# A new order for the start stage of a two-layer diffusion trunk: the first modulation group computed in halves

## The chip, the cores and the metric

The kernel runs on one core of one Trainium2 chip. The metric is the time of one execution in microseconds (us), measured on the device. TensorE multiplies matrices (PE; its weight loads are shown apart as PEld), VectorE (DVE), ScalarE (ACT) and GpSimd (POOL) compute, SyncE (SP) issues most transfers.

## The reference, cut to what matters

Two request groups (128 prompt tokens, 256 latent tokens) pass through two layers of width 1024, each a SwiGLU block, a token mixer and a second SwiGLU block. Before each block the tokens are normalised and modulated; `shift` and `scale` come from the conditioning vector by one large linear map:

```python
def modulate_norm(x, g, shift, scale):
    return rms_norm(x, g) * (1.0 + scale[:, None, :]) + shift[:, None, :]

m = (jax.nn.silu(cond) @ mod_w[l] + mod_b[l]).reshape(cond.shape[0], N_MOD, D_MODEL)
hf = modulate_norm(x, g[0], m[:, 0], m[:, 1])
x = x + FFN_RES * m[:, 2, None] * rms_norm(swiglu(hf, ffn_w1[l, 0], ffn_w2[l, 0]), g[1])
```

Only the very first use of this, up to the first three column units of the first `h @ w1`, lies in the code that is changed.

## The kernel before, in words

The 384 tokens are three tiles of 128 (tile 0 prompt, tiles 1 and 2 latent). All large products are fp32 in three passes: an operand is split into a high part (an ACT copy to fp32r, "hi", line 152 or 154 for weights, 431 for activations) and the rest (a DVE subtraction, "lo", lines 155 and 432). `mm3` (445 to 447) issues hi x hi, hi x lo of the activations, and lo of the weights x hi, so its third pass needs the weights' lo part.

Weights stream through four raw buffers of 1 MB; a unit is cast in two halves into three hi/lo buffers (`prep`). `release` gives a buffer back, `half` (`weights` in the start stage) casts the next one. With `"all"`, `prep` hands back four steps instead of doing them: hi and lo of the first 512 columns (`parts[u][0]`, `[1]`) and of the second 512 (`[2]`, `[3]`).

`start` (from line 721) handles what comes before the pipeline is full. It lies in a region of manual order (`order_begin`), in which every engine takes its instructions in the order of the program text. The code of `__init__` lies outside it. The stage consists of:

- statistics of each token tile: two ACT squares with a sum (331), then on DVE and ACT the reciprocal root (`rstd_of`, 310 to 322; the square root is ACT line 309), then the scaled tile `xn` (384 on DVE, 385 on ACT);
- `transposed(t)`: eight PE transposes (391) into two banks, copied out (765) by DVE and ACT;
- four modulation groups `g` of 256 columns each for shift and scale: `mods` (788, PE), `rows` (796, a DVE copy), `vectors` (801, PE, with the DVE steps 809 and 811 that make the vectors), `evac` (840 on DVE and 842 on ACT, then the split 431 and 432). Group `g` gives the row blocks k = 2g and 2g + 1 of the activations;
- `products(g, u)`: twelve matmuls of unit u for these two blocks, both halves (gate, up) of the unit. Groups 0 and 1 use the unit's first weight half (group 0 its first 512 columns, group 1 its second), groups 2 and 3 the second weight half;
- `keep_warm` (771): products of the identity with itself whose result nobody reads.

The order written out by hand after the transposes is, in short: `vectors(0)`, `evac(0)`, the casts of all three units, `products(0, 0)`, `products(0, 1)`, the second part casts, `mods(1)`, half of `products(0, 2)`, `vectors(1)`, `evac(1)`, the other half, `mods(2)`, `products(1, 0)`, `vectors(2)`, `evac(2)`, `next_weights(0)`, `products(1, 1)`, `next_weights(1)`, `products(1, 2)`, `mods(3)`, `next_weights(2)`, `products(2, 0)`, `vectors(3)`, `evac(3)`, `products(2, 1)`, `products(2, 2)`, and `products(3, u)`.

Of the kernel before, what the change touches and what calls it, by code (L numbers as in the profile page):

```python
# [19 lines left out]
P = 128  # L20
D = 1024
# [8 lines left out]

RAW_BUFS = 4
HALF_BUFS = 3
WARM, WARM2 = 10, 10
TAIL = 5


class Trunk:
    def __init__(self, ctx, tc, io):
        self.ctx, self.tc, self.nc, self.io = ctx, tc, tc.nc, io
        nc = self.nc  # L40
        pool = lambda name, bufs=1, **kw: ctx.enter_context(tc.tile_pool(name=name, bufs=bufs, **kw))
        self.cp = pool("const")
        self.sp = pool("small", 2)
        self.wp = pool("weights")
        self.pp = pool("psum", 1, space=bass.MemoryType.PSUM)
        self.dp = pool("scratch", 1, space=bass.MemoryType.DRAM)
        self.uid = 0

        const = lambda name, shape: self.cp.tile(shape, F32, tag=name, name=name)
        cc = const("cc", [P, KC, 2])  # L50
        nc.sync.dma_start(cc, io["cond"])
        self.x = const("x", [P, NT, D])
        for t in range(NT):
            src = io["x_prompt"] if t == 0 else io["x_sample"][(t - 1) * P : t * P]
            nc.sync.dma_start(self.x[:, t, :], src)
        self.nwT = const("nwT", [P, 6, KC])
        nc.gpsimd.dma_start(self.nwT, io["norm_pre"])
        self.mbT = const("mbT", [P, 6, 3, KC])
        nc.gpsimd.dma_start(self.mbT, io["mod_bT"])
        self.npT = const("npT", [P, 6, KC])  # L60
        nc.gpsimd.dma_start(self.npT, io["norm_post"])
        self.sel = const("sel", [P, 2])
        nc.gpsimd.dma_start(self.sel, io["sel"])
        self.csT = const("csT", [P, KC, 32])
        nc.vector.memset(self.csT, 0.0)
        self.cc = cc
        self.ident = const("ident", [P, P])
        make_identity(nc, self.ident)
        self.one = const("one", [P, 1])
        nc.vector.memset(self.one, 1.0)  # L70
        self.xh = self.cp.tile([P, KC, TOK], F32R, tag="xh", name="xh")
        self.xl = self.cp.tile([P, KC, TOK], F32R, tag="xl", name="xl")
        self.gates, self.shift, self.scale = {}, {}, {}
        self.gate_rows = {}
        self.cond_rows = None
# [295 lines left out]
    def stat_steps(self, t):  # L371

        nc = self.nc
        st = {}

        square, eps, sums = self.square_steps([self.x[:, t, 0:512], self.x[:, t, 512:1024]])

        def rstd():
            eps()
            st["z"] = self.rstd_of(**sums)  # L380

        def scale(tag="xn"):
            xn = self.cp.tile([P, D], F32, tag=tag, name=self.name("xn"))
            nc.vector.tensor_scalar(xn[:, 0:512], self.x[:, t, 0:512], st["z"], None, op0=ALU.mult)
            nc.scalar.activation(xn[:, 512:], self.x[:, t, 512:], AF.Copy, scale=st["z"])
            return xn

        return square, rstd, scale, eps
# [336 lines left out]
    def start(self, units):  # L725
# [3 lines left out]
        with self.tc.tile_pool(name="start", bufs=1, reuse_waits="tile") as tp:  # L729
            raw0 = {}  # L730

            def load(g):
                for v in range(2):
                    raw0[g, v] = tp.tile([P, KC, 256], F32, tag=f"m0_{g}_{v}", name=f"m0_{g}_{v}")
                    nc.sync.dma_start(raw0[g, v], io["mod_first"][g, v])
# [5 lines left out]
                    self.loaded += 1  # L741
                nc.sync.dma_start(self.raw[u][0][:, c0:c1], self.unit_src(units[u])[0][:, c0:c1])

            load(0)
            for g in range(2):
                for u in range(3):
                    load_part(u, 512 * g, 512 * (g + 1))
                load(g + 1)
            load_part(0, D, 2 * D)
            load(3)  # L750
            load_part(1, D, 2 * D)
# [22 lines left out]
            def squares(t):  # L774
                for h in (1, 0):
                    stats[t][0](h)

            vec = [self.mod_vec(v) for v in range(2)]
            self.shift[0], self.scale[0] = vec
            ws, sums, rowsof = {}, {}, {}  # L780
# [17 lines left out]
            def vectors(g, *vs):  # L798
                po = self.psum(1)
                for i in range(2 * vs[0], 2 * vs[-1] + 2):  # L800
                    nc.tensor.matmul(po[:, 2 * i : 2 * i + 2], rowsof[g][:, i * P : (i + 1) * P], self.sel,  # L801
                                     start=True, stop=True)
                for v in vs:
                    for j in range(2):
                        k = 2 * g + j
                        src = po[:, 4 * v + 2 * j : 4 * v + 2 * j + 2]
                        b = self.mbT[:, 0, v, k : k + 1]
                        if v == 0:
                            nc.vector.tensor_scalar(vec[0][:, :, k], src, b, None, op0=ALU.add)
                        else:  # L810
                            nc.vector.tensor_scalar(vec[1][:, :, k], src, b, self.nwT[:, 0, k : k + 1],
                                                    op0=ALU.add, op1=ALU.mult)

            squares(0), stats[0][1]()
            squares(1)
            xn0 = stats[0][2]()
            stats[1][1]()
            squares(2)
            xn1 = stats[1][2]("ptmp")
            nc.vector.tensor_scalar(self.nwT, self.nwT, RS, None, op0=ALU.mult)  # L820
            for j in range(6):
                nc.vector.tensor_scalar(self.mbT[:, j, 1, :], self.mbT[:, j, 1, :], 1.0, None, op0=ALU.add)
            stats[2][1]()
            transposed(0, xn0)
            xn2 = stats[2][2]()
            transposed(1, xn1)
            mods(0, 0)
            rows(0, 0)
            transposed(2, xn2)
            mods(0, 1)  # L830
            parts = {0: self.prep(1, "all")}
            parts[0][0]()
            rows(0, 1)
            banks = [self.psum(b) for b in (6, 7, 4, 5, 2, 3)]

            def evac(g, between=None):
                for j in range(2):
                    k = 2 * g + j
                    tmp = self.cp.tile([P, D], F32, tag=("xn", "ptmp")[j], name=self.name("xtmp"))[:, :TOK]
                    nc.vector.tensor_scalar(tmp[:, 0:P], xnT[:, k, 0:P], vec[1][:, 0, k : k + 1],  # L840
                                            vec[0][:, 0, k : k + 1], op0=ALU.mult, op1=ALU.add)
                    nc.scalar.activation(tmp[:, P:TOK], xnT[:, k, P:TOK], AF.Identity,
                                         bias=vec[0][:, 1, k : k + 1], scale=vec[1][:, 1, k : k + 1])
                    if between and j == 0:
                        between()
                    self.split(self.xh[:, k, :], self.xl[:, k, :], tmp)
# [1 line left out]
            def weights(u, h):  # L848
                ws[u, h] = self.half(units[u], h, ahead=0, hold=True)

            def products(g, u, gus=(0, 1)):
                for gu in gus:
                    for j in range(2):
                        k = 2 * g + j
                        c0 = (k % 4) * 256 + gu * P
                        w = ws[u, g // 2]
                        self.mm3(banks[2 * u + gu][:, :TOK], w[0][:, c0 : c0 + P], w[1][:, c0 : c0 + P],
                                 self.xh[:, k, :], self.xl[:, k, :], k == 0, k == KC - 1)
# [2 lines left out]
                self.release(units[u], 0)  # L861
                weights(u, 1)

            vectors(0, 0, 1)
            keep_warm(0, WARM2)
            evac(0, parts[0][1])
            for u in (1, 2):
                parts[u] = self.prep(1, "all")
                parts[u][0](), parts[u][1]()
            for u in range(3):  # L870
                weights(u, 0)
            products(0, 0)
            products(0, 1)
            for u in range(3):
                parts[u][2](), parts[u][3]()
            mods(1, 0), mods(1, 1), rows(1, 0, 1)
            products(0, 2, (0,))
            vectors(1, 0, 1)
            evac(1)
            products(0, 2, (1,))  # L880
            mods(2, 0), mods(2, 1), rows(2, 0, 1)
            products(1, 0)
            vectors(2, 0, 1)
            evac(2)
            next_weights(0)
            products(1, 1)
            next_weights(1)
            products(1, 2)
            mods(3, 0), mods(3, 1), rows(3, 0, 1)
            next_weights(2)  # L890
            products(2, 0)
            vectors(3, 0, 1)
            evac(3)
            products(2, 1)
            products(2, 2)
            self.prep(1)
            for u in range(3):
# [451 lines left out]
def host_arrays(i):  # L1349
# [10 lines left out]
    mw = np.asarray(i["mod_w"]).reshape(2, D, 9, 4, 2, P)  # L1360
    a["mod_w"] = f(mw.transpose(0, 2, 3, 5, 4, 1)).reshape(18, 4, P, 2048)
    first = np.asarray(i["mod_w"])[0, :, 0:2048].reshape(KC, P, 2, 4, 256)
    a["mod_first"] = f(first.transpose(3, 2, 1, 0, 4))
    mb = np.asarray(i["mod_b"]).reshape(6, 3, D)
    a["mod_bT"] = f(mb.reshape(6, 3, KC, P).transpose(3, 0, 1, 2))
    sel = np.zeros((4, 32, 2), np.float32)
# [84 lines left out]
```

## Time and profile before

| what | value |
|---|---|
| median of 3 runs | 1422.99 us (1421.85 to 1423.42) |
| the profiled execution, its own time | 1423.91 us |
| its span, first to last instruction | 1421.0 us |
| PE busy | 1405.4 us (99%) |
| DVE, ACT, POOL busy | 1021.1 us (72%), 614.5 us (43%), 29.0 us (2%) |
| share of PE in the chain that ended last | 93% |

In the rows further down the first number of a timeline row is the start, the second the duration, both in us; a row may stand for several instructions (x8), and the bracket at its end is the time for which the engine stood idle before it, with what ended the wait.

### The profile page before, as it was taken

Reading aid. Unit: us, or ns where it says so; the run is one execution under the profiler, and the core shown is the slowest. Engines: PE = TensorE matmul, PEld = TensorE weight load, DVE = VectorE, ACT = ScalarE, POOL = GpSimd, SP = SyncE. Lnnn points to the kernel's source line nnn. Section 1 sums busy time; section 2 is a strip of 40 time slices with the busy share of each in tenths; the row PEclk is TensorE's granted clock in tenths of the full one; section 3 lists DMA queues with packets and bytes.
Section 4 is the critical chain, followed back from the end, with each engine's and each line's share of the span. In section 5 each row is a group of like instructions: output and inputs, shape, how many; then the busy total and the mean of one; then the engine's idle time right before and its main releaser. Section 6 shows DMA issues by size and latency. Waiting matters only on the chain.

```text
span 1421.0 us, 19853 instructions
## 1 busy us (share of the span) xinstructions
PE 1405.4 (99%) x7747; PEld 1287.3 (91%) x7747; DVE 1021.1 (72%) x1798; ACT 614.5 (43%) x1051; POOL 29.0 (2%) x54
## 2 busy tenths in 40 slices
PE   8999999999999999999999999999999999999998
PEld 6999998889888999999889999988886899999886
DVE  5688868578997777986856889887678765555333
ACT  5533332363555633333355333323657663333322
POOL 0000000010000000000000000000100000000000
PEclk9999999999999999999999999999999999999999
DMA  9556555626545246655734566556350334444321
GB/s 372 212 214 259 195 207 221 260 100 247 201 149 199 96 175 235 237 207 182 275 135 153 203 233 241 198 217 251 107 205 30 119 119 152 173 150 178 130 107 45
DMA packets 38958, 262.58 MB, mean 185 GB/s; under 512 B 4816, under 2 KB 4976, under 8 KB 8784
## 3 DMA queue, kind: packets, MB, share of 16 engines
q1 hardware_dynamic: 35424, 243.29, 46.9%
q0 software_dynamic: 3440, 18.02, 3.5%
q8 instruction: 60, 0.98, 0.3%
q14 instruction: 34, 0.28, 0.1%
HBM read 259.01 MB, written 2.29 MB: 184 GB/s over the span
## 4 chain that ended last, share of the span: by engine, by line
PE 93%; DVE 3%; DMA 1%; ACT 1%; issue 1%; DVEq 0%; SPq 0%; ACTq 0%; POOLq 0%
PE psB L445 29%; PE psB L446 29%; PE psB L447 29%; PE psB L391 2%; PE psB L941 1%; PE psB L982 1%; DVE junkv L229 1%; DVE wlo L155 1%; DMA raw<-in_mod_w 1%; DMA csB<-crows 1%; PE psB L788 0%; ACT junk L331 0%; DMA x<-in_x_prompt 0%; PE psB L955 0%; PE psB L801 0%
## 5 line engine op out<-in xcount | busy, mean ns | idle before, releaser
L445 PE MATMUL psB<-xh,whi 128*128 128x384 f32 (+1 forms) x1536 | 517.0, 337 | 0.9 <-ACT qz L1085 0.7
L446 PE MATMUL psB<-xl,whi 128*128 128x384 f32 (+1 forms) x1536 | 512.3, 334 | 0.1
L447 PE MATMUL psB<-xh,wlo 128*128 128x384 f32 (+1 forms) x1536 | 512.0, 333 | 0.0
L155 DVE TENSOR_TENSOR wlo<-raw,whi 128x1024 fp32r<-128x1024 f32 (+2 forms) x286 | 336.6, 1186 | 121.0 <-ACT whi L152 119.2
L152 ACT CAST whi<-raw 128x1024 fp32r<-128x1024 f32 (+1 forms) x275 | 285.6, 1045 | 295.8 <-PE psB L446 132.2
L229 DVE CUSTOM_DVE_ANT_0 junkv<-raw,csB,mbT 128x1024 bf16<-128x1024 f32 x256 | 328.1, 1281 | 8.8 <-DMA csB<-crows 3.7
L445 PEld LDWEIGHTS psB<-xh,whi 128*128 128x128 f32 x1536 | 288.8, 188 | 5.7 <-issue 2.3
L446 PEld LDWEIGHTS psB<-xl,whi 128*128 128x128 f32 x1536 | 288.9, 188 | 1.6 <-DVE xl L432 0.9
L447 PEld LDWEIGHTS psB<-xh,wlo 128*128 128x128 f32 x1536 | 288.8, 188 | 0.0
L445 PE MATMUL psB<-whi,g 128*128 128x512 f32 x384 | 149.9, 390 | 0.0
L447 PE MATMUL psB<-whi,g 128*128 128x512 f32 x384 | 149.4, 389 | 0.0
L446 PE MATMUL psB<-wlo,g 128*128 128x512 f32 x384 | 149.4, 389 | 0.0
L431 ACT CAST g<-gt 128x384 fp32r<-128x384 f32 (+1 forms) x84 | 42.5, 505 | 201.3 <-DVE gt L622 201.3
L622 DVE TENSOR_TENSOR gt<-psB,sil 128x384 f32<-128x384 f32 (+1 forms) x88 | 48.1, 547 | 82.5 <-PE psB L447 74.7
L445 PEld LDWEIGHTS psB<-whi,g 128*128 128x128 f32 x384 | 72.1, 188 | 14.9
L447 PEld LDWEIGHTS psB<-whi,g 128*128 128x128 f32 x384 | 72.1, 188 | 14.9
L446 PEld LDWEIGHTS psB<-wlo,g 128*128 128x128 f32 x384 | 72.1, 188 | 14.7
L432 DVE TENSOR_TENSOR g<-gt,g 128x384 fp32r<-128x384 f32 (+1 forms) x84 | 46.1, 549 | 48.1 <-ACT g L431 48.1
L620 ACT ACTIVATE sil<-psB 128x384 f32<-128x384 f32 (+1 forms) x88 | 42.7, 485 | 86.5 <-PE psB L447 86.5
L445 PE MATMUL psB<-g,g 128*128 128x512 f32 x120 | 46.9, 391 | 0.0
L447 PE MATMUL psB<-g,g 128*128 128x512 f32 x120 | 46.7, 389 | 0.0
L446 PE MATMUL psB<-g,g 128*128 128x512 f32 x120 | 46.7, 389 | 0.0
(227 smaller groups left out, 1410.1 us busy)
## 6 DMA issues: line engine op xcount, KB each, us to landing
raw<-in_ffn_w SPq DMA_DIRECT2D x129, 1024.0 KB, 4.9
raw<-in_mod_w SPq DMA_DIRECT2D x64, 1024.0 KB, 4.9
raw<-in_ev_in SPq DMA_DIRECT2D x10, 1024.0 KB, 4.8
m<-in_mod_first SPq DMA_DIRECT2D x8, 1024.0 KB, 13.1
gate<-gscr POOLq DMA_DIRECT2D x6, 1024.0 KB, 5.0
csB<-crows POOLq DMA_DIRECT2D x4, 1024.0 KB, 7.4
raw<-in_ev_out SPq DMA_DIRECT2D x4, 1024.0 KB, 5.1
raw<-in_od_out SPq DMA_DIRECT2D x4, 1024.0 KB, 4.9
```

The costliest lines, as they stand in the source:

```text
L152: nc.scalar.copy(hi, src)
L155: sub = lambda hi=hi[:, c], lo=lo[:, c], src=src[:, c]: nc.vector.tensor_tensor(lo, src, hi.bitcast(F32), ALU.subtract)
L229: nc.vector.tensor_tensor_reduce(junk[:, :D], self.raw[i][0][:, kk * D : (kk + 1) * D], self.csB[:, c, :], 1.0, self.mbT[:, s, kind, k : k ...
L391: self.nc.tensor.transpose(out, src, self.ident)
L431: self.nc.scalar.copy(hi, src)
L432: sub = lambda: self.nc.vector.tensor_tensor(lo, src, hi.bitcast(F32), ALU.subtract)
L445: nc.tensor.matmul(out, ah, bh, start=first, stop=False)
L446: nc.tensor.matmul(out, ah, bl, start=False, stop=False)
L447: nc.tensor.matmul(out, al, bh, start=False, stop=last)
L620: nc.scalar.activation(sil[:, :n], pg[:, :n], AF.Silu)
L622: nc.vector.tensor_tensor(gt[:, :n], pu[:, :n], sil[:, :n], ALU.mult)
L941: nc.tensor.matmul(sp[:, :384], qk(i, e, t + 1), kk(i, e)[0], start=True, stop=True)
```

## The change

Five things are changed, all of them ahead of 53.4 us or in the host's layout of the weights.

1. The first modulation group is split into two column blocks. `mod_first0` holds it as four pieces of 512 KB, loaded by `load_half` between the first weight pieces; `mods_half`, `rows_half` and `vectors_half` do one block each, the first one behind all three transposes.
2. The squares of tile 2 are shared: DVE does one half (`tensor_tensor_reduce`), ACT the other, and an addition joins them ahead of `rstd_of`.
3. The scaling of `nwT` and the six additions to `mbT` move from DVE in `start` to POOL in `__init__`, ahead of `make_identity`.
4. Some `keep_warm` products stand between the steps: 10, 2, 2, 2 and 4 in place of 10 and 10.
5. The order behind the first vectors is a new one, in which products of group 0 are done by column block.

```diff
+        nc.gpsimd.tensor_scalar(self.nwT, self.nwT, RS, None, op0=ALU.mult)
+        for j in range(6):
+            nc.gpsimd.tensor_scalar(self.mbT[:, j, 1, :], self.mbT[:, j, 1, :], 1.0, None, op0=ALU.add)
...
+            def load_half(j):
+                for v in range(2):
+                    raw0[0, v, j] = tp.tile([P, KC, P], F32, tag=f"m0h_{v}_{j}", name=f"m0h_{v}_{j}")
+                    nc.sync.dma_start(raw0[0, v, j], io["mod_first0"][j, v])
...
-            load(0)
-            for g in range(2):
-                for u in range(3):
-                    load_part(u, 512 * g, 512 * (g + 1))
-                load(g + 1)
+            load_half(0)
+            load_part(0, 0, 512)
+            load_half(1)
+            load_part(1, 0, 512)
+            load_part(2, 0, 512)
+            load(1)
+            for u in range(3):
+                load_part(u, 512, 1024)
+            load(2)
...
+            def square_shared():
+                junk = self.cp.tile([P, D + 192], BF16, tag="junkv", name=self.name("junkv"))
+                xs = [self.x[:, 2, 512 * h : 512 * h + 512] for h in range(2)]
+                nc.vector.tensor_tensor_reduce(junk[:, 0:512], xs[1], xs[1], 1.0 / D, zero, ALU.mult, ALU.add, ss2[1])
+                junk = self.cp.tile([P, 512], BF16, tag="junk", name=self.name("junk"))
+                nc.scalar.activation(junk, xs[0], AF.Square, scale=1.0 / 32.0, accum_out=ss2[0])
...
+            def mods_half(v, j):
+                if v == 0:
+                    sums[0, j] = self.psum(0)
+                for kk in range(2):
+                    for q in range(4):
+                        nc.tensor.matmul(sums[0, j][32 * q : 32 * q + 32, P * v : P * v + P],
+                                         self.csT[:, 2 * q + kk, :], raw0[0, v, j][:, 2 * q + kk, :],
+                                         start=(kk == 0), stop=(kk == 1))
...
             squares(0), stats[0][1]()
             squares(1)
             xn0 = stats[0][2]()
+            square_shared()
             stats[1][1]()
-            squares(2)
             xn1 = stats[1][2]("ptmp")
-            nc.vector.tensor_scalar(self.nwT, self.nwT, RS, None, op0=ALU.mult)
-            for j in range(6):
-                nc.vector.tensor_scalar(self.mbT[:, j, 1, :], self.mbT[:, j, 1, :], 1.0, None, op0=ALU.add)
-            stats[2][1]()
+            nc.vector.tensor_tensor(ss2[1], ss2[1], ss2[0], ALU.add)
+            z2 = self.rstd_of(ss2[1])
             transposed(0, xn0)
-            xn2 = stats[2][2]()
+            keep_warm(0, 2)
+            xn2 = stats[2][2]("xn", z2)
             transposed(1, xn1)
-            mods(0, 0)
-            rows(0, 0)
+            keep_warm(0, 2)
             transposed(2, xn2)
-            mods(0, 1)
             parts = {0: self.prep(1, "all")}
             parts[0][0]()
-            rows(0, 1)
+            mods_half(0, 0)
+            mods_half(1, 0)
+            rows_half(0)
+            parts[0][1]()
+            keep_warm(1, 2)
+            vectors_half(0)
             banks = [self.psum(b) for b in (6, 7, 4, 5, 2, 3)]
...
-            vectors(0, 0, 1)
-            keep_warm(0, WARM2)
-            evac(0, parts[0][1])
+            evac(0, None, (0,))
+            keep_warm(0, 4)
+            mods_half(0, 1), mods_half(1, 1)
+            weights(0, 0)
+            products(0, 0, js=(0,))
+            rows_half(1)
+            vectors_half(1)
             for u in (1, 2):
                 parts[u] = self.prep(1, "all")
                 parts[u][0](), parts[u][1]()
-            for u in range(3):
                 weights(u, 0)
-            products(0, 0)
-            products(0, 1)
+                products(0, u, js=(0,))
+                if u == 1:
+                    evac(0, None, (1,))
+            products(0, 0, js=(1,))
+            mods(1, 0), mods(1, 1), rows(1, 0, 1)
+            products(0, 1, js=(1,))
+            vectors(1, 0, 1)
+            evac(1)
             for u in range(3):
                 parts[u][2](), parts[u][3]()
-            mods(1, 0), mods(1, 1), rows(1, 0, 1)
-            products(0, 2, (0,))
-            vectors(1, 0, 1)
-            evac(1)
-            products(0, 2, (1,))
+            products(0, 2, js=(1,))
+            products(1, 0)
             mods(2, 0), mods(2, 1), rows(2, 0, 1)
-            products(1, 0)
+            products(1, 1)
             vectors(2, 0, 1)
             evac(2)
+            products(1, 2)
             next_weights(0)
-            products(1, 1)
+            products(2, 0)
+            mods(3, 0), mods(3, 1), rows(3, 0, 1)
             next_weights(1)
-            products(1, 2)
-            mods(3, 0), mods(3, 1), rows(3, 0, 1)
-            next_weights(2)
-            products(2, 0)
+            products(2, 1)
             vectors(3, 0, 1)
             evac(3)
-            products(2, 1)
+            next_weights(2)
             products(2, 2)
```

## Rows read from the trace of the kernel before

**Rows 1.** Windows of PE: stretch, its length, busy time, granted clock, DMA share, GB/s

```profile
20.00:53.40 33.40, 33.40 (x261) 1.00 0.83 325
53.40:1400.00 1346.60, 1343.54 (x7318) 1.00 0.50 181
```

**Rows 2.** Timeline of PE and its weight loads, start stage

```profile
4.17 3.86 PE L771 MATMUL psB<-ident 128*128 128x128 f32 x20 [4.17 <-POOL ident masks.py:199]
...
12.77 1.09 PE L391 MATMUL psB<-ident,xn 128*128 128x128 f32 x8 [0.17 <-DVE xn L384]
...
15.87 2.48 PE L771 MATMUL psB<-ident 128*128 128x128 f32 x20
18.11 0.42 PE L445 MATMUL psB<-xh,whi 128*128 128x384 f32 x1
...
23.59 1.93 PE L788 MATMUL psB<-m,csT 128*32 128x256 f32 x32
...
26.61 0.95 PE L801 MATMUL psB<-sel,rows 128*128 128x2 f32 x8
...
42.91 0.42 PE L445 MATMUL psB<-xh,whi 128*128 128x384 f32 x1
...
53.40 0.35 PE L445 MATMUL psB<-xh,macc 128*128 128x384 f32 x1
...
13.79 0.59 PEld L788 LDWEIGHTS psB<-m,csT 128*32 128x32 f32 x16 [0.17 <-DVE rows L796]
```

**Rows 3.** Timeline of DVE and of ACT, the evacuation of group 1

```profile
29.34 0.56 DVE L432 TENSOR_TENSOR xl<-xtmp,xh 128x384 fp32r<-128x384 f32 x1 [0.77 <-ACT xh L431]
...
28.80 0.51 ACT L431 CAST xh<-xtmp 128x384 fp32r<-128x384 f32 x1
...
30.25 0.51 ACT L431 CAST xh<-xtmp 128x384 fp32r<-128x384 f32 x1 [0.43 <-DVE xtmp L840]
```

**Rows 4.** Timeline of ACT and of DVE, the weights' casts

```profile
21.99 1.96 ACT L154 CAST whi<-raw 128x512 fp32r<-128x512 f32 x3 [1.67 <-DMA raw<-in_ffn_w]
...
36.96 2.95 ACT L152 CAST whi<-raw 128x1024 fp32r<-128x1024 f32 x3
...
22.64 2.03 DVE L155 TENSOR_TENSOR wlo<-raw,whi 128x512 fp32r<-128x512 f32 x3 [1.52 <-ACT whi L154]
...
38.05 2.36 DVE L155 TENSOR_TENSOR wlo<-raw,whi 128x1024 fp32r<-128x1024 f32 x2 [0.40 <-ACT whi L152]
```

**Rows 5.** Timeline of ACT and DVE, roots of tiles 1 and 2

```profile
8.62 0.28 ACT L309 ACTIVATE rq<-ss 128x1 f32<-128x1 f32 x1
8.81 0.61 ACT L331 ACTIVATE junk<-x 128x512 bf16<-128x512 f32 x1
...
10.79 0.28 ACT L309 ACTIVATE rq<-ss 128x1 f32<-128x1 f32 x1
...
11.55 0.16 DVE L322 SCALAR_TENSOR_TENSOR rz<-ra,ry 128x1 f32<-128x1 f32 x1
```

**Rows 6.** First weight pieces (SP issues, their landing); ACT around its wait

```profile
L742 SPq DMA_DIRECT2D raw<-in_ffn_w x3: 496/502/532, 3.6 to 4.7; - x3
...
DMA to landing us min/median/max: 10.5/11.2/11.3
...
16.68 0.60 ACT L842 ACTIVATE xtmp<-xnT,mv,mv 128x256 f32<-128x256 f32 x1 [1.68 <-DVE mv L811]
...
19.18 1.14 ACT L154 CAST whi<-raw 128x512 fp32r<-128x512 f32 x2
```

**Rows 7.** The modulation bias: its issue on POOL, KB and median landing

```profile
L59 POOL DMA_DIRECT2D mbT<-in_mod_bT x1: 547/547/547, 1.9 to 1.9; - x1
...
mbT<-in_mod_bT POOLq DMA_DIRECT2D x1, 72.0 KB, 5.0
```

**Rows 8.** Timeline of DVE in the first mixer, outside the region

```profile
364.67 0.54 DVE L950 TENSOR_TENSOR p<-psB,bias 128x384 f32<-128x384 f32 x1
365.13 0.74 DVE L917 TENSOR_SCALAR p<-p,r 128x384 f32<-128x384 f32 x2
```

More of the change, by code (lines that the diff above doesn't have):

```diff
@@ L32 @@
 HALF_BUFS = 3
-WARM, WARM2 = 10, 10
+WARM = 10
 TAIL = 5
@@ L380, in rstd, with scale @@
             st["z"] = self.rstd_of(**sums)
-        def scale(tag="xn"):
+        def scale(tag="xn", z=None):
+            if z is not None:
+                st["z"] = z
             xn = self.cp.tile([P, D], F32, tag=tag, name=self.name("xn"))
@@ L776, in squares @@
                     stats[t][0](h)
+            zero = self.sp.tile([P, 1], F32, tag="l", name=self.name("l"), bufs=4)
+            nc.vector.memset(zero, 0.0)
+            ss2 = [self.sp.tile([P, 1], F32, tag="l", name=self.name("l"), bufs=4) for _ in range(2)]
+            def square_shared():
[4 more added lines that the diff above has]
+                nc.scalar.activation(junk, xs[0], AF.Square, scale=1.0 / 32.0, accum_out=ss2[0])
             vec = [self.mod_vec(v) for v in range(2)]
@@ L804, in vectors, with set_vec, rows_half, vectors_half @@
                     for j in range(2):
[L805 to L812, printed above, removed]
+                        set_vec(v, 2 * g + j, po[:, 4 * v + 2 * j : 4 * v + 2 * j + 2])
+            def set_vec(v, k, src):
+                b = self.mbT[:, 0, v, k : k + 1]
+                if v == 0:
+                    nc.vector.tensor_scalar(vec[0][:, :, k], src, b, None, op0=ALU.add)
+                else:
+                    nc.vector.tensor_scalar(vec[1][:, :, k], src, b, self.nwT[:, 0, k : k + 1],
+                                            op0=ALU.add, op1=ALU.mult)
+            def mods_half(v, j):
+                if v == 0:
+                    sums[0, j] = self.psum(0)
[4 more added lines that the diff above has]
+                                         start=(kk == 0), stop=(kk == 1))
+            def rows_half(j):
+                rowsof[0, j] = tp.tile([P, 256], F32, tag="rowsh", name=self.name("rows"))
+                nc.vector.tensor_copy(rowsof[0, j], sums[0, j][:, 0:256])
+            def vectors_half(j):
+                po = self.psum(1)
+                for v in range(2):
+                    nc.tensor.matmul(po[:, 2 * v : 2 * v + 2], rowsof[0, j][:, v * P : (v + 1) * P], self.sel,
+                                     start=True, stop=True)
+                for v in range(2):
+                    set_vec(v, j, po[:, 2 * v : 2 * v + 2])
             squares(0), stats[0][1]()
@@ L816, in start, with evac @@
             xn0 = stats[0][2]()
+            square_shared()
             stats[1][1]()
-            squares(2)
             xn1 = stats[1][2]("ptmp")
-            nc.vector.tensor_scalar(self.nwT, self.nwT, RS, None, op0=ALU.mult)
-            for j in range(6):
-                nc.vector.tensor_scalar(self.mbT[:, j, 1, :], self.mbT[:, j, 1, :], 1.0, None, op0=ALU.add)
-            stats[2][1]()
+            nc.vector.tensor_tensor(ss2[1], ss2[1], ss2[0], ALU.add)
+            z2 = self.rstd_of(ss2[1])
             transposed(0, xn0)
-            xn2 = stats[2][2]()
+            keep_warm(0, 2)
+            xn2 = stats[2][2]("xn", z2)
             transposed(1, xn1)
-            mods(0, 0)
-            rows(0, 0)
+            keep_warm(0, 2)
             transposed(2, xn2)
-            mods(0, 1)
             parts = {0: self.prep(1, "all")}
             parts[0][0]()
-            rows(0, 1)
+            mods_half(0, 0)
[4 more added lines that the diff above has]
+            vectors_half(0)
             banks = [self.psum(b) for b in (6, 7, 4, 5, 2, 3)]
-            def evac(g, between=None):
-                for j in range(2):
+            def evac(g, between=None, js=(0, 1)):
+                for j in js:
                     k = 2 * g + j
@@ L849, in weights, with products @@
                 ws[u, h] = self.half(units[u], h, ahead=0, hold=True)
-            def products(g, u, gus=(0, 1)):
+            def products(g, u, gus=(0, 1), js=(0, 1)):
                 for gu in gus:
-                    for j in range(2):
+                    for j in js:
                         k = 2 * g + j
@@ L1362, in host_arrays @@
     first = np.asarray(i["mod_w"])[0, :, 0:2048].reshape(KC, P, 2, 4, 256)
-    a["mod_first"] = f(first.transpose(3, 2, 1, 0, 4))
+    first = first.transpose(3, 2, 1, 0, 4)
+    a["mod_first"] = f(first)
+    a["mod_first0"] = f(first[0].reshape(2, P, KC, 2, P).transpose(3, 0, 1, 2, 4))
     mb = np.asarray(i["mod_b"]).reshape(6, 3, D)
```

## The prediction

> **What bounds the kernel.** I began with the busy times of the page (PE 99%), then read PE in windows. From 20.0 to 53.4 us PE is busy for all of the 33.40 us, and in the next 1346.60 us it idles for 3.06 [rows 1]. So the kernel is bound by PE from 20 us on. Whatever the start stage loses is added to the end, as only those 3 us of later idle time could take anything up. Next I read PE's timeline: the last transposes start at 12.77, the first product at 18.11, the first 24 products are done when the modulation of group 1 starts at 23.59, and the stage ends when the product after it starts, at 53.40 [rows 2]. From 42.91 to 53.40 PE does sixty products, 0.175 us each. A group's modulation takes 1.9 us, its eight vector products 0.95 [rows 2].
>
> The question is how long PE waits in the new order. For this I read the chain behind a group's vectors, counted from the end of the vector products (26.61 + 0.95 = 27.56): the first block's hi part is there after 1.75 us (28.80 + 0.51), its lo part after 2.34, the second block's hi part after 3.20 [rows 3], its lo part some 0.6 later. On ACT a hi cast of 512 columns takes 0.65 us, one of 1024 columns 0.98; on DVE the lo part takes 0.68 and 1.18 [rows 4].
>
> **The order of an engine is that of the text.** ACT idled for 1.68 us up to 16.68, waiting for the vectors. The first pieces of all three units had landed by 16.0 (4.7 + 11.3), yet units 1 and 2 were cast only at 19.18, behind the evacuation, where the text has them [rows 6]. A cast behind an `evac` in the text thus waits for that `evac`.
>
> **The new order, step by step.** In the kernel before, 24 matmuls or a modulation stand between each `vectors` and the products that need it. Now:
>
> - `products(1, 0)` follows `vectors(1)` after six products, so PE arrives 0.9 us behind the vectors (PE goes on 0.15 ahead of their modelled end). It needs the second 512 columns of unit 0, and those casts stand behind `evac(1)` on ACT: 3.20 + 0.65 = 3.85. PE waits 3.0. The lo part follows at 4.55, while the third pass is due at 4.25: 0.3 more. Sum 3.3.
> - `products(2, 0)` follows `vectors(2)` after twelve products, at 1.95. The next weight half is cast behind `evac(2)`: hi at 3.20 + 0.98 = 4.2, lo at 5.4. PE waits 2.25 and 0.85, sum 3.1. Before, 24 products and a modulation lay here.
> - `products(2, 1)`: the lo part of unit 1 stands on DVE behind `rows(3)`, which waits for PE's `mods(3)`. From the end of `mods(3)` it takes 0.7 + 1.2 us, while PE has two passes to do (0.3): 1.6.
> - `products(2, 2)` follows `vectors(3)` directly, at -0.15, and its weights are cast behind `evac(3)`: hi at 4.2, lo at 5.4. PE waits 4.35 and 0.8, sum 5.15.
>
> These four make 13.2 us.
>
> **The part up to the first 24 products.** Sharing tile 2's squares takes one square off ACT, but puts the other ahead of tile 1's root. Two squares and a scaling (0.6) fill 8.81 to 10.79, so a square costs about 0.7, and that root moves from 8.62 to 9.35. From a root to its result takes 0.92 us (10.79 to 11.71) [rows 5], so tile 1 is ready at 10.3. Tile 2's addition, its epsilon and its root follow tile 1's scaling (0.4, then 0.25 each): root at 11.2, result at 12.1 in place of 11.7. DVE's half of the squares (nearest row: an elementwise step of 512 columns, 0.68 [rows 4]) lies beside ACT's and costs nothing unless tile 2 lands after 8.6. The transposes of tile 2 thus start about 13.2, 0.45 late; bounds: 0.4 early (no delay by ACT's order) to 1 late.
>
> The steps moved to POOL cost nothing: the bias lands at 1.9 + 5.0 = 6.9 [rows 7] and is wanted at 16.5. Their half microsecond on DVE was beside the ACT queue, so nothing is gained. The two additional SP issues bring no more bytes, and every piece stands in nearly the same place of the queue. SP's loads of the next units wait for raw buffers that the casts of the second halves free; they become late by about as much as PE does, so nothing waits for them.
>
> A pair of `mods_half` is 32 passes of half the width. Lower bound: half of 1.93, 1.0 (width decides); upper: 1.93 (the count decides). I take 1.2, nearest to the weight loads, 16 in 0.59 [rows 2]. [...] The row of 32 at 60 ns each cannot tell the two apart, since these are twice as wide.
>
> So: transposes to 14.25, modulation to 15.5, rows to 15.95, four vector products to 16.5, two vector steps to 16.95, chain to the first block's hi and lo at 18.15 and 18.7. PE meanwhile does its filling and the second block's modulation, so the first product starts at 18.6 in place of 18.11. Six products and the second vectors last to 20.1. Unit 1's lo part stands on DVE behind these vectors: wait of 0.9. Unit 2's hi part stands on ACT behind the second block (0.7), its lo part on DVE (0.3). The 24 products are done at 25.1, **1.6 us later** than before.
>
> **Sum.** 1.6 + 13.2 = 14.8, less some 0.4 of small gaps that PE now spends inside the waits: **+14.4 us**. The filling costs nothing itself (20 products before and after). Against the profiled execution, 1423.91 us, that is **1438.3 us**; it was 0.9 above the median of the runs, 1422.99, so by the median it would be 1437.4.
>
> **Rivals.**
>
> [...]
>
> *The identity is late.* In POOL's text order the identity comes behind the scaled bias, so at 6.9 plus seven small steps (0.1 to 0.3 each) and 0.5: at 8.1 to 9.4, and with the filling of 3.9, two tiles' transposes (1.1 each) and two pairs of filling (0.45 each) tile 2's start at 15.1 to 16.4 in place of 13.2: 1.9 to 3.2 more, 1440.2 to 1441.5. Against it: this code is outside the region of manual order, and there an instruction is put ahead of one that waits: the multiplication at 365.13 follows its reciprocal in the text, but the next item's addition at 364.67 was put between [rows 8].
>
> *The order isn't kept.* If the scheduler ran the casts when their data lie ready, the weights would be there and products could fill the waits. What then stays is tile 2's delay of 0.45 less four vector products and two vector steps (0.5 and 0.3): 1423.5, no change. It decides where ACT casts ahead of an `evac`; rows 6 speak against it.
>
> **Chances.** Forecast as worked out 0.60 (1436 to 1440), clock 0.22, identity 0.09, order not kept 0.04, other sizes 0.05. The low end: transposes without delay (-0.9), narrow passes (-0.2), lo parts half hidden (-1.5), and something of the later 3 us takes up the rest: 1435. The high end takes in the clock at 3 us and 1.3 for `mods_half` at its upper bound, 1442.6, rounded to 1443. About 0.2% (2.8 us) can be told from no change; faster 0.02, within 0.03, slower 0.95.
>
> **What would show it.** In the changed kernel's PE timeline: a wait of 3 us on an ACT cast (154) after `vectors(1)`, 2.3 on a cast (152) after `vectors(2)`, 1.6 on DVE 155 after `mods(3)`, over 4 on 152 after `vectors(3)`; the product behind the stage starting near 68 us in place of 53.4; no new idle time after it. [...] The forecast is wrong if ACT's casts of the second halves stand ahead of `evac(2)` and `evac(3)`, or if PE has other products to do there.

## The result, and the profile after

The changed kernel took 1443.44 us (median of 4 runs, 1442.43 to 1444.13) against 1422.47 for the kernel before: a ratio of 1.0148, 95% interval 1.0135 to 1.0160. That is 21.0 us slower. 1438.3 was forecast, with a range of 1435 to 1443. The direction was right; the time is 5.1 us above the forecast and 0.4 us outside the range, and the loss of 21.0 us is 6.6 us more than the +14.4 of the sum.

The timeline of PE in the changed kernel (lines 396 transposes, 845 `mods_half`, 450 to 452 the three passes of a product, 813 `mods`, 826 `vectors`):

```profile
13.39 1.09 PE L396 MATMUL psB<-ident,xn 128*128 128x128 f32 x8 [0.59 <-DVE xn L389]
14.41 1.08 PE L845 MATMUL psB<-m0h,csT 128*32 128x128 f32 x32
...
18.87 0.44 PE L450 MATMUL psB<-xh,whi 128*128 128x384 f32 x1
...
21.70 0.44 PE L452 MATMUL psB<-xh,wlo 128*128 128x384 f32 x1 [0.64 <-DVE wlo L158]
...
23.08 0.44 PE L450 MATMUL psB<-xh,whi 128*128 128x384 f32 x1 [0.42 <-ACT whi L157]
...
25.75 1.93 PE L813 MATMUL psB<-m,csT 128*32 128x256 f32 x32
...
33.48 0.45 PE L450 MATMUL psB<-xh,whi 128*128 128x384 f32 x1 [2.61 <-ACT whi L157]
...
46.90 0.44 PE L450 MATMUL psB<-xh,whi 128*128 128x384 f32 x1 [2.02 <-ACT whi L155]
...
48.16 0.45 PE L452 MATMUL psB<-xh,wlo 128*128 128x384 f32 x1 [0.65 <-DVE wlo L158]
...
55.52 0.44 PE L452 MATMUL psB<-xh,wlo 128*128 128x384 f32 x1 [1.41 <-DVE wlo L158]
...
57.36 0.95 PE L826 MATMUL psB<-sel,rows 128*128 128x2 f32 x8
62.80 0.69 PE L450 MATMUL psB<-xh,whi 128*128 128x384 f32 x1 [4.50 <-ACT whi L155]
...
74.42 0.34 PE L450 MATMUL psB<-xh,macc 128*128 128x384 f32 x1
```

Read against [rows 2]: the 24 products that ended at 23.59 end at 25.75, 2.2 us later. Then come four waits, each named by what ended it: a late hi cast (155, 157) or a late lo part (158). The product behind the stage starts at 74.42 in place of 53.40, 21.0 us later: the whole loss lies ahead of it. The waits are its first part. The windows of PE in the changed kernel (stretch, length, busy time, granted clock, DMA share, GB/s) show the second:

```profile
20.00:30.00 10.00, 8.83 (x72) 1.00 1.03 416
...
35.00:37.00 2.00, 2.00 (x7) 0.50 1.06 430
37.00:39.60 2.60, 2.60 (x34) 0.74 0.61 239
39.60:44.60 5.00, 5.00 (x36) 1.00 0.00 2
...
48.40:51.00 2.60, 2.60 (x10) 0.54 0.64 205
51.00:53.50 2.50, 2.50 (x35) 0.80 0.50 206
53.50:57.40 3.90, 2.49 (x18) 1.00 0.23 48
...
62.80:69.00 6.20, 5.95 (x17) 0.50 0.45 169
...
74.40:1420.00 1345.60, 1343.23 (x7317) 1.00 0.49 181
```

The granted clock is a share of full speed. In windows of 0.25 us over 34.50 to 40.00, 46.50 to 54.00 and 61.00 to 70.00 it reads 0.50 or 1.00, but for the six in which it changes (0.68 to 0.99); so a value between the two is here the mean of a stretch with both. It reads 0.50 in every such window from 35.00 to 38.25, from 48.75 to 52.00 and from 62.25 to 69.00, so with three of the four waits (the one of 1.6 us, in the stretch from 53.50, is followed by 1.00); in [rows 1] the clock is 1.00 throughout. At 0.50 the products start 0.32 us apart, at 1.00 0.17. Busy time times the clock's missing share gives 1.0 + 0.7, 1.2 + 0.5 and 3.0: **6.4 us lost at the lower clock**. In the last line PE idles for 2.4 us, against 3.1 in the nearly equal stretch of [rows 1], and the spans of the two profiled executions differ by 20.3 us (1441.3 and 1421.0). So at most 0.7 us was given back later; one execution of each kernel cannot tell that from the spread between runs.

The waits themselves are read from the timeline. A product's pass is due 0.175 us after the pass before it (0.32 at the lower clock behind the last wait), and the first one behind the vector products 0.8 us after their start, as in the kernel before.

| ahead of | hi part late by | lo part late by | sum | forecast |
|---|---|---|---|---|
| `products(1, 0)` | 2.8 | 0.3 | 3.1 | 3.3 |
| `products(2, 0)` | 2.2 | 0.8 | 3.0 | 3.1 |
| `products(2, 1)` | 0 | 1.6 | 1.6 | 1.6 |
| `products(2, 2)` | 4.6 | 0.5 | 5.1 | 5.15 |

Sum 12.8, against 13.2 forecast. With 2.2 ahead of them and 6.4 for the clock this makes 21.4; the small gaps that PE had in the kernel before, and that now lie inside the waits, may account for the difference to 21.0, which no row shows apart.

That the casts wait behind the evacuation stands in ACT's timeline of the changed kernel (436 is the hi part of the activations, 157 and 155 the casts):

```profile
32.40 0.51 ACT L436 CAST xh<-xtmp 128x384 fp32r<-128x384 f32 x1 [0.43 <-DVE xtmp L889]
32.81 1.65 ACT L157 CAST whi<-raw 128x512 fp32r<-128x512 f32 x3
...
58.91 0.60 ACT L891 ACTIVATE xtmp<-xnT,mv,mv 128x256 f32<-128x256 f32 x1 [11.12 <-DVE mv L837]
...
61.29 0.51 ACT L436 CAST xh<-xtmp 128x384 fp32r<-128x384 f32 x1 [0.73 <-DVE xtmp L889]
61.71 1.04 ACT L155 CAST whi<-raw 128x1024 fp32r<-128x1024 f32 x1
```

Unit 2's second half had been in its raw buffer for a long time (its load was issued at 23.5 at the latest, and from 39.60 to 44.60 the DMA share is 0.00), and ACT stood idle for 11 us ahead of `evac(3)`, whose first step is the row at 58.91. The cast begins the moment the evacuation is through.

### The profile page after: what moved, and what is told of

Read it like the earlier page. It is cut to its first block, busy times and chain, and to the rows that moved or that the text cites. A ratio compares the mean times of both kernels' runs of the same rounds, so it can differ in the third digit from the quotient of the medians.

```text
span 1441.3 us, 19921 instructions
## 1 busy us (share of the span) xinstructions
PE 1413.6 (98%) x7779; PEld 1292.9 (90%) x7779; DVE 1021.1 (71%) x1794; ACT 613.5 (43%) x1049; POOL 30.9 (2%) x61
## 4 chain that ended last, share of the span: by engine, by line
PE 92%; DVE 4%; ACT 1%; issue 1%; DMA 1%; DVEq 0%; SPq 0%; ACTq 0%; POOLq 0%
PE psB L452 29%; PE psB L450 29%; PE psB L451 29%; PE psB L396 2%; PE psB L995 1%; DVE junkv L232 1%; DVE wlo L158 1%; PE psB L1036 1%; DMA csB<-crows 1%; PE psB L813 0%; DMA x<-in_x_prompt 0%; ACT junk L334 0%; ACT xh L436 0%; PE psB L1009 0%; DVE xl L437 0%
```

## The experiments

The theory: the new order puts casts behind `evac` in ACT's and DVE's queues; PE waits for them (13 us), and the waits bring its clock down (6 us); the early part costs some 2 us. The rivals: the halves and their transfers; PE's own order; products that are slow for another reason than the clock. Ratios and differences are against the runs of the kernel before that were taken beside each experiment (medians 1422.39 and 1422.25 us).

**The early part alone.** The order from group 1 on is that of the kernel before; halves, shared squares, POOL steps, filling and the first 24 products stay as changed.

```diff
 products(0, 0, js=(1,))
+parts[u][2](), parts[u][3]() for all u, then as before:
+mods(1), products(0, 1, js=(1,)), vectors(1), evac(1), products(0, 2, js=(1,)), mods(2), products(1, 0), ...
```

> The changed kernel with the order of the kernel before from group 1 on (parts 1 to 4 of the change and the first 24 products by column block stay). Theory (the waits of the new order and the clock that they bring down cost nearly all): the product behind the stage starts at 55 to 56 us against 53.40 before and 74.42 in the changed kernel, granted clock 1.00 from 20 us on, time 1424 to 1425. Rival (the halves, the shared squares and their transfers carry a large share): 1428 or more, with new waits ahead of 26 us.

Measured: 1423.93 us (10 runs), ratio 1.0012 (1.0003 to 1.0022), 1.5 us slower. PE's timeline, then one window of the same execution:

```profile
12.85 1.09 PE L396 MATMUL psB<-ident,xn 128*128 128x128 f32 x8 [0.59 <-DVE xn L389]
...
21.17 0.45 PE L452 MATMUL psB<-xh,wlo 128*128 128x384 f32 x1 [0.64 <-DVE wlo L158]
...
22.55 0.46 PE L450 MATMUL psB<-xh,whi 128*128 128x384 f32 x1 [0.42 <-ACT whi L157]
...
56.37 0.34 PE L450 MATMUL psB<-xh,macc 128*128 128x384 f32 x1
...
22.50:24.50 2.00, 1.95 (x6) 0.59 1.02 424
```

The time is at the low edge of the theory's 1424 to 1425. The stage ends later than expected (56.37), and the clock was not 1.00: it fell at 22.8 in this execution, which took 1424.89 us, the longest of the ten, behind the two short waits. In the changed kernel's profile the same two waits did not bring it down (1.00 from 20.00 to 30.00). A profile further down (squares back on ACT) has the two waits, a clock of 1.00 and nearly the same loss, so the early part's 1.5 us doesn't need the clock. It is a small share of the 21.

**The casts written ahead.** PE's order is that of the change; each line with a plus is moved up from its place there.

```diff
+parts[u][2](), parts[u][3]()          (ahead of mods(1))
 products(1, 0)
+next_weights(0)
 mods(2, 0), mods(2, 1), rows(2, 0, 1)
 products(1, 1)
 vectors(2, 0, 1)
 evac(2)
+next_weights(1)
 products(1, 2)
+next_weights(2)
```

> The changed kernel with PE's order untouched, but every late cast written ahead of the evacuation that it stood behind. Theory (casts queued behind evac on ACT and DVE make the waits): the waits on casts go, what stays is the evacuation chain ahead of products(1, 0) (2 us) and products(2, 0) (1 us), time 1427 to 1429, up to 1431 if one of these brings the clock down. Rival (PE's own order is at fault, whatever the casts do): 1437 or more.

Measured: 1428.61 us, ratio 1.0046 (1.0031 to 1.0061). Waits of PE (who waited, for whom; us in total, times, the longest):

```profile
PE psB L450 <- ACT xh L436: 1.4, 4, 0.6
...
PE psB L451 <- DVE xl L437: 0.6, 4, 0.2
PE psB L450 <- ACT whi L157: 0.4, 1, 0.4
```

Moving the casts alone gives back 14.8 of the 21 us (1443.44 - 1428.61). The waits that stay are for the activations, as expected, and the only late casts are those of the early part, ahead of 23.5 us. PE's own order costs the rest, 4.7 us over the early part alone; counted from when a pass was due, the waits for the activations are 2.1 us ahead of and in `products(1, 0)`, 1.0 in `products(2, 0)` and, not foreseen, 1.0 in `products(3, 0)`.

**Filling in the waits.** Idle products keep PE at work; the casts come as late as in the change.

```diff
 products(0, 2, js=(1,))
+keep_warm(0, 11)
 products(1, 0)
...
 products(1, 2)
+keep_warm(0, 8)
...
+keep_warm(1, 5)
 products(2, 1)
...
+keep_warm(0, 19)
 products(2, 2)
```

> The changed kernel with 11, 8, 5 and 19 idle products of the identity inside its four long waits; the waits stay as long. Theory (the slow stretches are the clock, and it falls because PE stands idle): granted clock 1.00 from 33 to 70 us, products at 0.17 us throughout, time 1436 to 1438. Rival (the products behind the waits are slow for another reason, such as the transfers that run then): slow stretches stay, 1443 to 1445.

Measured: 1437.54 us (4 runs, three from 1437.11 to 1437.84 and one of 1440.34), ratio 1.0111 (1.0096 to 1.0126). Windows of PE:

```profile
33.00:50.00 17.00, 15.92 (x136) 1.00 0.48 187
50.00:70.00 20.00, 18.93 (x128) 1.00 0.42 145
```

Work that nobody reads makes the kernel 5.9 us faster (1443.44 - 1437.54), and the granted clock stays at 1.00. The slow stretches were the clock, and here idle time brought it down: with PE idle in the waits it read 0.50 behind three of them, with the waits filled 1.00 from 33 to 70 us. What is left, 15.2 us over the kernel before (1437.54 - 1422.39), is the waits and the early part: the forecast's sum (14.4) with the clock held. The run of 1440.34 has a mean granted clock of 0.998, the other three 0.999 to 1.000; so the filling may not have held the clock everywhere in it.

**One cast late.** The kernel before with one line moved.

```diff
-next_weights(2)
 products(2, 0)
 vectors(3, 0, 1)
 evac(3)
+next_weights(2)
 products(2, 1)
 products(2, 2)
```

> The kernel before with one line moved: the cast of unit 2's second half stands behind evac(3) in place of ahead of products(2, 0); PE's order is the same. Theory (a cast waits for the evac that is ahead of it in the text): PE waits 2.3 us for the hi part and 0.8 for the lo part ahead of products(2, 2), 1425.5, and 1426.5 to 1428 if the clock falls there. Rival (ACT does the cast when its data are there): no wait, 1422 to 1423.

Measured: 1427.98 us, ratio 1.0039 (1.0024 to 1.0053), runs from 1425.37 to 1429.61. PE's timeline and two windows:

```profile
47.26 0.45 PE L445 MATMUL psB<-xh,whi 128*128 128x384 f32 x1 [2.02 <-ACT whi L152]
48.52 0.44 PE L447 MATMUL psB<-xh,wlo 128*128 128x384 f32 x1 [0.64 <-DVE wlo L155]
...
49.00:51.00 2.00, 2.00 (x8) 0.50 0.68 201
51.00:53.00 2.00, 2.00 (x10) 0.66 0.80 328
```

One line of text costs 5.6 us (1427.98 - 1422.39). The wait is that of the theory: 2.2 and 0.8, counted from when the passes were due, for 2.3 and 0.8.

**The same with filling in the wait.**

```diff
 products(2, 1)
+keep_warm(0, 9)
 products(2, 2)
```

> The kernel before with unit 2's cast behind evac(3), and nine idle products of the identity in the wait ahead of products(2, 2). Theory (that wait costs 3 us itself and the rest of the 5.6 us was the clock): granted clock 1.00 behind it, 1425 to 1425.6, runs within 1 us of each other. Rival (the slow stretch comes from the late cast's traffic): 1427 to 1429 as without them.

Measured: 1425.37 us (10 runs, 1425.16 to 1425.67), ratio 1.0021 (1.0012 to 1.0031). PE's window behind the wait:

```profile
48.00:52.00 4.00, 3.36 (x20) 1.00 0.48 160
```

The wait alone costs 3.1 us (1425.37 - 1422.25), the clock 2.6 at the medians (1427.98 - 1425.37). With the clock held the runs lie within 0.5 us; without, they spread over 4.2.

**The reorder alone.** The kernel before with part 5 from group 1 on.

```diff
 products(0, 0)
-products(0, 1)
+products(0, 1, js=(0,))
+products(0, 2, js=(0,))
+mods(1, 0), mods(1, 1), rows(1, 0, 1)      (and on as in the change)
```

> The kernel before with part 5 of the change alone, from group 1 on (halves, shared squares, POOL steps and filling as before). Theory (the reorder's waits cost 13 us and the clock 6, the rest of the change 1.5): 1441 to 1442.5, slow stretches behind the same three waits. Rival (the parts need each other, the halves make the reorder dear): 1436 or less.

Measured: 1441.51 us, ratio 1.0134 (1.0120 to 1.0149). PE's timeline:

```profile
31.45 0.69 PE L445 MATMUL psB<-xh,whi 128*128 128x384 f32 x1 [2.61 <-ACT whi L154]
...
45.70 0.44 PE L445 MATMUL psB<-xh,whi 128*128 128x384 f32 x1 [2.01 <-ACT whi L152]
...
54.34 0.44 PE L447 MATMUL psB<-xh,wlo 128*128 128x384 f32 x1 [1.40 <-DVE wlo L155]
...
61.33 0.69 PE L445 MATMUL psB<-xh,whi 128*128 128x384 f32 x1 [4.20 <-ACT whi L152]
...
73.20 0.35 PE L445 MATMUL psB<-xh,macc 128*128 128x384 f32 x1
```

The same waits to within 0.3 us, and 19.3 of the 21 us (1441.51 - 1422.25). Early part (1.5) and reorder (19.3) make 20.8 of the change's 21.0.

**Squares back on ACT**, in the kernel with the early part alone.

```diff
-square_shared()
 stats[1][1]()
+squares(2)
 xn1 = stats[1][2]("ptmp")
-nc.vector.tensor_tensor(ss2[1], ss2[1], ss2[0], ALU.add)
-z2 = self.rstd_of(ss2[1])
+stats[2][1]()
```

> The kernel with the early part alone, with tile 2's squares back on ACT. By the prediction's step (sharing the squares delays tile 2 by 0.4 us) tile 2's transposes start 0.4 us sooner than in the kernel with the early part alone (12.85 there) and the time falls by as much, to 1423.5. Rival (sharing is neutral, since x lands late enough to set both): within 0.15 us of 12.85, time unchanged.

Measured: 1423.66 us (10 runs), ratio 1.0012 (1.0002 to 1.0021). PE's timeline, then two windows of the same execution:

```profile
12.75 1.09 PE L396 MATMUL psB<-ident,xn 128*128 128x128 f32 x8 [0.73 <-DVE xn L389]
...
18.23 0.44 PE L450 MATMUL psB<-xh,whi 128*128 128x384 f32 x1
...
54.91 0.35 PE L450 MATMUL psB<-xh,macc 128*128 128x384 f32 x1
...
20.00:30.00 10.00, 8.83 (x70) 1.00 1.03 415
30.00:56.00 26.00, 26.00 (x197) 1.00 0.71 278
```

The rival holds: 0.10 us between 12.85 and 12.75, and no difference in time that can be told. But the reason is not the one written beside it: the next row, of ACT in the kernel with the shared squares (`early_only`), shows tile 2's root at 10.95, only 0.16 behind [rows 5], and a root of 0.20 us in place of 0.28.

```profile
10.95 0.20 ACT L310 ACTIVATE rq<-rv 128x1 f32<-128x1 f32 x1
```

This profile also prices the early part at a clock of 1.00: the first product starts 0.1 us after that of the kernel before (18.23 against 18.11), the stage ends 1.5 us later (54.91 against 53.40). So the early part's loss lies behind the first product, where PE waits for the two casts.

**Halves with the old order and early casts.** The hi casts of units 1 and 2 stand ahead of the first evacuation, the second half's modulation takes the place of filling, and the rest is ordered as before. The edit in short, with filling of 3 and 2 products where the change has 2 and 4:

```diff
+for u in range(3): parts[u][0]()          (ahead of mods_half(0, 0))
 vectors_half(0)
+evac(0, parts[1][1], (0,))
+mods_half(0, 1), mods_half(1, 1)
+rows_half(1)
+products(0, 0, js=(0,))
+vectors_half(1), parts[2][1](), evac(0, None, (1,))
+products(0, 1, js=(0,)), products(0, 2, js=(0,))
+all parts[u][2](), parts[u][3](), then mods(1) and products by the order of before
```

> Halves and shared squares kept, the order from group 1 on as before, the hi casts of units 1 and 2 ahead of the first evacuation, and the second half's modulation in place of filling. Theory (what is left of the loss ahead of 26 us are waits on casts behind the vectors and a clock drop behind them): no wait of PE over 0.2 us from the first product on, the product behind the stage starts at 53.0 to 53.6, 1421.8 to 1422.8, no difference from the kernel before that can be told. Rival (the halves themselves cost): 1424 or more.

Measured: 1422.59 us (11 runs, 1421.9 to 1422.88), ratio 1.0001 (0.9992 to 1.0010). PE's timeline:

```profile
18.23 0.44 PE L450 MATMUL psB<-xh,whi 128*128 128x384 f32 x1
18.82 0.45 PE L451 MATMUL psB<-xl,whi 128*128 128x384 f32 x1 [0.15 <-DVE xl L437]
...
53.27 0.34 PE L450 MATMUL psB<-xh,macc 128*128 128x384 f32 x1
```

From the first product on PE has one wait left, of 0.15 us, and the stage ends at 53.27 against 53.40. So the halves are not dear in themselves, and with the two waits the loss of the early part is gone. Casts, modulation, filling and order were moved together here, so this run alone doesn't tell them apart. The halves bring nothing that can be measured either: no version tried beats the kernel before.

## Why the prediction was right and where it was wrong

- **Which waits, for what, how long:** right in all four, to 0.3 us. The argument from [rows 6], that an engine's order is that of the text, carried it, and moving the casts alone gave 14.8 us back (waits and clock together).
- **"These four make 13.2 us", sum +14.4:** right as the time with the clock held: 15.2 measured with filling in the waits.
- **The step that failed: the clock was left out of the sum.** It had a chance of 0.22 and, at the upper end of the range, 3 us. No run shows that term as the price in all; in its place the runs showed 6.4 us by the windows and 5.9 by the run with filling. The granted clock fell to 0.50 three times, with the waits of 3.1, 3.0 and 5.1 us, at a cost of 1.7, 1.7 and 3.0. PE worked at 0.50 for 3.3, 3.3 and 6.2 us there, with products 0.32 us apart in place of 0.17.
- **The filling of [rows 2] gives no price for the clock.** Twenty passes behind 4.17 us of idle time took 3.86 us, twenty behind work 2.48, a difference of 1.4. But the granted clock over the first twenty, in the windows of the kernel before, reads 1.00 (rows below), so no run shows that this difference is the clock's.

```profile
4.50:5.00 0.50, 0.50 (x4) 1.00 1.03 369
...
7.50:8.00 0.50, 0.50 (x6) 1.00 1.16 425
```

- **The range was missed by only 0.4 us, and that is luck.** Its base, the profiled execution (1423.91), is 1.4 us above the median of the kernel before that stands beside the result (1422.47), and its upper end held 1.3 for `mods_half`. No run shows that term; a pair took 1.08 us, less than the 1.2 in the sum.
- **The first 24 products 1.6 us later:** 2.2 in this execution. The first tile landed later in it (ACT's first square at 5.46, in the early part alone at 4.92), 0.5 us that the kernel with the early part alone did not show. Without it the first product comes 0.2 us later than before, where 0.5 was forecast. The waits on units 1 and 2 were 0.8 and 0.6 + 0.3 for 0.9 and 0.7 + 0.3 forecast.
- **Tile 2 delayed 0.45 by the shared squares:** wrong; 0.1. The step from tile 1's scaling to tile 2's root was taken as 0.9 us and measured 0.77 (10.18 to 10.95), and the new root is shorter.
- **A pair of `mods_half` at 1.2:** 1.08, by its row, or 34 ns for each of its 32 passes (1.08 / 32), against 60 ns at twice the width (1.93 / 32, [rows 2]). So the width counts nearly in full here: half of 1.93 would be 0.97.
- **Rival "identity late":** it did not happen. POOL's timeline of the changed kernel has the identity ahead of the scaled bias, which costs POOL 0.24 us a piece:

```profile
3.86 0.29 POOL masks.py:199 TENSOR_SCALAR_AFFINE_SELECT ident<-ident 128x128 f32<-128x128 f32 x1
...
7.28 1.44 POOL L66 TENSOR_SCALAR mbT<-mbT 128x8 f32<-128x8 f32 x6 [1.24 <-DMA mbT<-in_mod_bT]
```

- **Rival "order isn't kept":** did not happen either, as ACT's rows above show.

## What to carry to other kernels

In a hand-written order every cast has two places: that of PE's product and that in ACT's and DVE's queues; write it ahead of the evacuation that PE will wait for anyway, not beside the product that needs it (14.8 of the 21.0 us here). Count waits of TensorE like these twice: the wait itself, and the products that may run at a lower clock behind it. Here that was a granted 0.50 and 1.7 to 3.0 us with the waits of 3.0 to 5.1 us, and nothing with the one of 1.6. Where such a wait can't be removed, idle products inside it are worth their few lines (5.9 us here, 2.6 in the case of one wait).

## What was not expected of the hardware

- The clock's fall was not fixed by the kernel. The two short waits of the early part (0.64 and 0.42 us of idle time by the rows) went with a granted 0.59 behind them (22.50 to 24.50) in the profiled execution of the early part alone, and with 1.00 (20.00 to 30.00) in the changed kernel's, whose text is the same up to there. The kernel with one late cast spread over 4.2 us between runs, and over 0.5 with the wait filled; its lowest run, 1425.37, is the median with the wait filled.
- From 7 to 22.5 us the clock of the early part alone stayed at 1.00 although PE idled there (for 0.59 us of the 3 from 12 to 15), and so did that of the changed kernel behind its wait of 1.6 us (1.00 from 53.50 to 57.40).
